# Column tiles by pairs in seven block products instead of eight, in a hybrid decoder step

## The chip, the cores and the metric

The kernel runs on one core of one Trainium2 chip. The metric is device time in microseconds (us). Engines are named as in the profile: PE is TensorE (PEld is its weight load), DVE is VectorE, ACT is ScalarE, POOL is GpSimd and SP is SyncE. SP issues most weight loads, POOL most other DMAs; each issues its queue in order.

## The reference

One layer of a decoder that runs stick-breaking attention and a gated short convolution side by side. The input is 528 prompt tokens (16 learned meta tokens and 512 others) and 32 sample tokens (8 sequences of 4), 560 in all, 2048 wide.

```python
h = rmsnorm(x, g_pre)
q, k, v, ga, cb, cc, ch, gc, ma, mc = jnp.split(h @ w_in, split_offsets(), axis=-1)
a = attend(q, k, v, b_sb).reshape(bsz, t, D_ATTN) * jax.nn.silu(ga)
u = cc * ch
u_ext = jnp.concatenate([conv_hist.astype(u.dtype), u], axis=1)
c = cb * causal_conv(u_ext, w_conv, b_conv) * jax.nn.silu(gc)
merged = (jax.nn.sigmoid(ma + b_gate[:D_MODEL]) * (a @ w_pa)
          + jax.nn.sigmoid(mc + b_gate[D_MODEL:]) * (c @ w_pc))
y = x + rmsnorm(merged @ w_out, g_post)
```

`w_in` is 2048 x 12288 float32: the eight parts q to gc are 1024 wide, ma and mc 2048 each. `w_pa` and `w_pc` are 1024 x 2048, `w_out` is 2048 x 2048. Attention has 8 heads of 128. Prompt queries read earlier prompt keys. The queries of a sample sequence read 512 past keys, in four pages of 128 that a page table names, and its earlier new keys. `A[t,s] = sigmoid(z_ts) * prod_{s<j<t} (1 - sigmoid(z_tj))` takes the place of a softmax. The convolution is depthwise with three taps. Outputs are y, the new keys and values, and the last two rows of u, for prompt and samples.

## The kernel before

**Products.** Every large product is made in two-part float32: an operand is split into `hi`, a rounded fp32r copy (ACT), and `lo`, the rest (DVE subtracts). Three matmuls, hi by hi, lo by hi and hi by lo, give one product. `weights` (L180) loads a block of 1024 x 128 of a weight on SP's queue into a `raw` buffer, ACT casts it (L188) and DVE subtracts (L189). `raw` has three buffers (L67), `hi` and `lo` four each (L68). `gemm_into` (L193) runs over two ranges of tokens, over all contraction tiles of 128, and over the three matmuls (L201). The activations h are stationary in SBUF as `h_hi` and `h_lo` (16 contraction tiles x 560 tokens each), with the tokens on the columns of the matmul. `proj` (L216) computes a column tile, 128 columns of h @ w_in: two weight blocks, 2 x 16 x 3 = 96 matmuls of 272 tokens or so, into two of three `mm` banks of PSUM.

**Stages.** (1) Norm of x, split of h (L98 to L244). (2) The gate `ga` of all heads, then head by head k, v, q and prompt attention (L335); the attention of a head runs beside the projections of the next, its result goes to `a_scr` in DRAM. (3) The output gates: 16 x 2 column tiles of ma and mc, a sigmoid each, both to `gate_scr` in DRAM (L659). (4) The conv: `conv_in` (L481) makes u and the three taps of a channel tile out of its cc and ch tiles; a second loop (L683) multiplies with silu(gc) and cb, and keeps the eight results in SBUF as `c_raw`. Tile 0 is made ahead, behind the last head (L516), before that head's pool closes. In the second loop a is read back from `a_scr` and split to `a_hl` (L697), two tiles in each of its last four rounds. (5) `c_raw` is split to `c_hl` (L705), which takes the memory of `h_hi`. Then for two output tiles at a time a @ w_pa and c @ w_pc, with the gate read back from `gate_scr` (L715 to L732); the merged result is split as m. (6) The output product: 288 tokens with weights stationary (L773), the others with m stationary (L812), with norm and residual. It begins on the DMA of x rows into memory that `a_hl` leaves.

**Decode.** The attention of the samples is a generator, `decode_steps` (L537), of which `dec_step` runs a piece. Logits: for each of 32 pages a key tile of 128 keys x 1024; for two of four tokens DVE multiplies a whole page by the query row, broadcast to all partitions (L553), and ACT sums by head (L556); for the other two DVE multiplies and sums by head (L560). One page per column tile of the gates. Then softplus, running sums and exponentials, and the value pages through PE (L631), between the conv's tiles. Its result `a_s` goes into the sample columns of `a_hl`.

**Order.** The program is written for a scheduler: instructions have the priority of their place in the text, each engine's queue is laid out ahead by a simulated timeline, later work fills the gaps of earlier work once its buffers are free, and buffers of a tag go round among their tiles. A pool that is opened after another is closed uses the same memory, so its first writes wait for the last readers there. The order in a queue is then fixed.

The lines that the change and the prediction's steps touch are those named, and the pool sizes:

```python
wraw = ctx.enter_context(tc.tile_pool(name="wraw", bufs=3))   # L67
whl = ctx.enter_context(tc.tile_pool(name="whl", bufs=4))     # L68
```

## Time and profile before

| what | value |
|---|---|
| median of 3 runs | 1734.3 us (1733.22 to 1734.79) |
| span of the profiled execution | 1736.9 us, 2.6 us above that median |
| PE busy | 1706.4 us, 12764 matmuls |
| DVE, ACT, POOL busy | 842.8, 744.7, 202.2 us |
| heads, up to the last output | about 66 to 543 us |
| gates, decode logits beside the first 250 us | 543 to 943 us |
| conv and value pages | 943 to 1332 us |
| w_pa, w_pc | 1332 to about 1529 us |
| output product, norm | about 1529 to 1737 us |
| HBM read, written | 225.42, 22.36 MB |

The span goes from the first to the last instruction of one profiled execution. A profiled execution has no other time of its own, so the span stands for it. [...]

### The profile page before, as it was taken

How to read it: one execution, taken by the hardware profiler on the slowest of the kernel's cores; microseconds unless marked ns; L12 is line 12 of the kernel's file. 1: busy time of each engine (PE TensorE's matmuls, PEld its weight loads, DVE VectorE, ACT ScalarE, POOL GpSimd, SP SyncE). 2: the span in 40 equal slices, each digit the busy share in tenths (PEclk: the TensorE clock that was granted, in tenths of full speed). 3: DMA queues.
4: the chain of work that ended last, by engine and by line, in shares of the span. 5: the costliest groups of instructions: out<-in, count | busy, mean ns of one | idle time of the engine just before them, and what ended most of it. 6: DMA issues, size and time to landing. Idle time of an engine off the chain costs nothing.

```text
span 1736.9 us, 32151 instructions
## 1 busy us (share of the span) xinstructions
PE 1706.4 (98%) x12764; PEld 1637.0 (94%) x12764; DVE 842.8 (49%) x2092; ACT 744.7 (43%) x2026; POOL 202.2 (12%) x345
## 2 busy tenths in 40 slices
PE   5999999999999999999999999999999999999997
PEld 4999999999999999999999878899999999999986
DVE  7322554554445999996123222242224554444464
ACT  4322555455454999886223111132223222244543
POOL 5000222122111111111001111010000000000010
PEclk9999999999999999999999999999999999999999
DMA  6333333333325777774343444343233444567584
GB/s 191 94 110 116 88 99 93 87 88 98 99 82 192 247 257 253 248 244 148 111 120 102 166 160 149 121 139 91 80 98 85 137 127 133 164 166 184 174 260 153
DMA packets 302057, 249.87 MB, mean 144 GB/s; under 512 B 9181, under 2 KB 272145, under 8 KB 298721
## 3 DMA queue, kind: packets, MB, share of 16 engines
q1 hardware_dynamic: 278992, 161.89, 32.0%
q0 software_dynamic: 22912, 85.91, 14.2%
q8 instruction: 100, 1.64, 0.4%
q14 instruction: 51, 0.42, 0.1%
q10 hardware_dynamic: 2, 0.01, 0.0%
HBM read 225.42 MB, written 22.36 MB: 143 GB/s over the span
## 4 chain that ended last, share of the span: by engine, by line
PE 95%; DVE 2%; DMA 2%; ACT 0%; issue 0%; SPq 0%; POOLq 0%; POOL 0%; ACTq 0%; DVEq 0%
PE mm L201 83%; PE z L631 2%; PE z L830 2%; PE mm L830 2%; PE z L450 1%; DMA raw<-in_w_out 1%; PE o L460 1%; PE z L396 1%; PE o L830 1%; DMA raw<-in_w_in 1%; DVE hn L164 0%; PE tp L830 0%; PE tp L316 0%; DVE h_lo L177 0%; PE z L785 0%; DVE rtmp L120 0%
## 5 line engine op out<-in xcount | busy, mean ns | idle before, releaser
L201 PE MATMUL mm<-h_hi,wlo 128*128 128x272 f32 (+4 forms) x3072 | 894.1, 291 | 0.0
L201 PE MATMUL mm<-h_hi,whi 128*128 128x272 f32 (+4 forms) x3072 | 892.9, 291 | 0.0
L201 PE MATMUL mm<-h_lo,whi 128*128 128x272 f32 (+4 forms) x3072 | 888.1, 289 | 0.3 <-DVE h_lo L177 0.2
L201 PEld LDWEIGHTS mm<-h_hi,whi 128*128 128x128 f32 x3072 | 580.7, 189 | 9.3 <-issue 6.7
L201 PEld LDWEIGHTS mm<-h_hi,wlo 128*128 128x128 f32 x3072 | 580.0, 189 | 4.1 <-issue 3.4
L201 PEld LDWEIGHTS mm<-h_lo,whi 128*128 128x128 f32 x3072 | 579.2, 189 | 4.8 <-issue 3.4
L189 DVE TENSOR_TENSOR wlo<-raw,whi 128x1024 fp32r<-128x1024 f32 x252 | 308.4, 1224 | 493.7 <-ACT whi L188 492.3
L188 ACT CAST whi<-raw 128x1024 fp32r<-128x1024 f32 x256 | 269.0, 1051 | 518.0 <-PE mm L201 499.8
L556 ACT ACTIVATE junk<-pr 128x128 f32<-128x128 f32 x512 | 150.7, 298 | 7.1 <-DVE pr L553 4.3
L560 DVE CUSTOM_DVE_ANT_0 prod<-page,qb 128x128 f32<-128x128 f32 x512 | 116.2, 285 | 1.0 <-DMA qb<-q_scr 1.0
L201 PE MATMUL mm<-m,whi 128*128 128x288 f32 x512 | 105.8, 301 | 0.0
L556 ACT ACTIVATION_READ_ACCUMULATOR junk<-pr 128x1 f32 x512 | 97.2, 190 | 0.0
L201 PE MATMUL mm<-c_hl,whi 128*128 128x272 f32 x512 | 96.8, 287 | 0.0
L201 PE MATMUL mm<-a_hl,whi 128*128 128x272 f32 x512 | 96.7, 288 | 0.0
L201 PEld LDWEIGHTS mm<-m,whi 128*128 128x128 f32 x512 | 84.0, 193 | 0.0
L553 DVE TENSOR_TENSOR pr<-page,qb 128x1024 f32<-128x1024 f32 x64 | 78.0, 1220 | 6.2 <-ACT junk L556 5.7
L201 PEld LDWEIGHTS mm<-c_hl,whi 128*128 128x128 f32 x512 | 80.7, 188 | 0.0
L201 PEld LDWEIGHTS mm<-a_hl,whi 128*128 128x128 f32 x512 | 80.5, 189 | 0.0
L201 PE MATMUL mm<-m,wlo 128*128 128x288 f32 x256 | 76.6, 299 | 0.0
L201 PE MATMUL mm<-c_hl,wlo 128*128 128x272 f32 x256 | 74.2, 290 | 0.0
L201 PE MATMUL mm<-a_hl,wlo 128*128 128x272 f32 x256 | 73.9, 289 | 0.0
L804 DVE TENSOR_TENSOR wlo<-raw,whi 128x1024 fp32r<-128x1024 f32 x32 | 39.1, 1224 | 38.4 <-ACT whi L803 37.9
(289 smaller groups left out, 1641.6 us busy)
## 6 DMA issues: line engine op xcount, KB each, us to landing
raw<-in_w_in SPq DMA_DIRECT2D x192, 512.0 KB, 3.9
raw<-in_w_out SPq DMA_DIRECT2D x64, 512.0 KB, 4.0
qb<-q_scr POOLq DMA_DIRECT2D x16, 1024.0 KB, 7.1
page<-in_cache_k POOLq DMA_DIRECT2D x32, 512.0 KB, 6.0
page<-in_cache_v POOLq DMA_DIRECT2D x32, 512.0 KB, 5.4
gate_scr<-gt POOLq DMA_DIRECT2D x16, 544.0 KB, 4.6
gt<-gate_scr POOLq DMA_DIRECT2D x16, 544.0 KB, 5.1
raw<-in_w_pa SPq DMA_DIRECT2D x16, 512.0 KB, 3.9
```

The costliest lines, as they stand in the source:

```text
L188: act.copy(hi, raw)
L189: lo_eng.tensor_sub(lo, raw, hi.bitcast(F32))
L201: pe.matmul(o, lhsT=w, rhs=r[:, t0:t1], start=(k == 0 and n == 0), stop=(k == nk - 1 and n == 2))
L396: pe.matmul(zt[:m, c0:c0 + n], lhsT=l[:, s0:s0 + m], rhs=r[:, ts:ts + n], start=(c0 == 0 and i == 0), stop=(i == 2), skip_group_check=True)
L450: pe.matmul(o, lhsT=l, rhs=x, start=False, stop=(i == len(ops) - 1), skip_group_check=True)
L460: pe.matmul(ot[:, ts - NMETA:ts - NMETA + n], lhsT=l[:m, st, :], rhs=x[:m, c0:c0 + n], start=False, stop=(g == GROUPS[-1] and i == 2), ski ...
L553: dve.tensor_mul(pr, kt, qb[0][:, t, :])
L556: act.activation(junk, pr[:, h * P:(h + 1) * P], AF.Copy, accum_out=z_all[:, pg, b, h, t:t + 1])
L560: dve.tensor_tensor_reduce(out=prod, in0=kt[:, h * P:(h + 1) * P], in1=qb[t // 2][:, t % 2, h * P:(h + 1) * P], scale=1.0, scalar=0.0, op0 ...
L631: pe.matmul(po[hf][32 * j:32 * (j + 1), :], lhsT=lhs, rhs=rhs, start=(pg == 0), stop=(pg == NPG), tile_position=(0, 32 * j), skip_group_ch ...
L804: dve.tensor_sub(lo, raw, hi.bitcast(F32))
L830: pe.matmul(po[i], lhsT=l, rhs=r, start=(k == 0 and q == 0), stop=(k == KD - 1 and q == 2))
```

## The change

**Tokens.** They are laid out in two halves of 280, each with 8 meta tokens ahead of 272 others. In every product the two ranges then have the same width: 280, 274 (272 and two before) or 272. The meta tokens are put back in front where keys and values are copied out (`nparts`).

**Pairs.** `pair(c, n)` computes two neighbouring column tiles for both halves of the tokens as a 2 x 2 block product: two blocks of contraction (1024 each) by two column tiles of the weight, and two blocks of contraction by two halves of the tokens. It uses the Winograd form with seven block products instead of eight. A block product is 8 contraction tiles x 3 matmuls. Sums of weight blocks are made on DVE (four passes over 128 x 1024 a pair, partly in place), and seven blocks are split instead of four. Sums of token blocks are made once (`diff`, `t_split`): three new split blocks of 8 x 274 columns, and the block (0, 1) of h is overwritten by a difference. The partial results accumulate in three PSUM banks with copies between (ACT, and two subtractions of DVE). The conv's cc, ch, gc, cb go by pairs (16 pairs), then ma and mc from tile 2 on (14 pairs). Four gate tiles, 0 and 1 of ma and mc, stay whole and run while the token sums are made.

**Order.** After the heads: four gate tiles, four conv pairs of channels (`conv_pair`), gate pairs. The heads' pool is closed before the first of these. Conv results go to `c_scr` in DRAM and are read back to `c_hl` when h is done. Then all 16 tiles of c @ w_pc, each multiplied by its gate and written back to `gate_scr`; then a is read back and split to `a_hl`; then all 16 tiles of a @ w_pa, with the sum. These loads share two buffers (tag `gt` of the pool `g3`).

**Decode.** Key pages are loaded in halves of 512 columns, once for each two tokens (twice the key traffic), in 32 steps of four half pages; a step has either the ACT sums or the DVE sums. `dec_group` runs a step behind four of every five pairs, 24 in all; the eight others and the rest of the decode run in the w_pc loop, two steps a tile. `v_new` goes through DRAM.

**Sizes.** `wraw` 3 to 5, `whl` 4 to 3, and the SBUF kept for DMA descriptors is 4096 bytes a partition.

```diff
-    wraw = ctx.enter_context(tc.tile_pool(name="wraw", bufs=3))
-    whl = ctx.enter_context(tc.tile_pool(name="whl", bufs=4))
+    wraw = ctx.enter_context(tc.tile_pool(name="wraw", bufs=5))
+    whl = ctx.enter_context(tc.tile_pool(name="whl", bufs=3))
...
+    def pair(c, n):
+        c1, c2, k1, k2 = slice(c, c + P), slice(c + P, c + 2 * P), slice(0, 1024), slice(1024, 2048)
+        w11, w21, w22, w12 = (w_load(win[k, m]) for k, m in ((k1, c1), (k1, c2), (k2, c2), (k2, c1)))
...
+        def product(o, w, rhs, start, stop):
+            hi, lo = w
+            for k in range(8):
+                rh, rl = rhs(k)
+                for m, (l, r) in enumerate(((hi, rh), (hi, rl), (lo, rh))):
+                    pe.matmul(o, lhsT=l[:, k, :], rhs=r, start=(start and k == 0 and m == 0),
+                              stop=(stop and k == 7 and m == 2), skip_group_check=True)
...
+        x, q, y = mm_ps()[:, :n], mm_ps()[:, :n], o_ps()[:, :n]
+        s = sp2.tile([P, 8, P], F32, name="s")
...
+        product(x, w_split(w11), rb(0, 0), True, False)
+        dve.tensor_add(s, w21, w22)
+        product(q, w_split(s), rb(0, 1), True, False)
+        act.activation(y, x, AF.Copy, scale=-1.0)
+        dve.tensor_add(s, s, w11)
+        product(y, w_split(s), rt(0), False, False)
+        s5 = tmp("s5")
+        act.copy(s5, q)
+        product(x, w_split(w12), rb(1, 0), False, True)
+        s2 = tmp("s2")
+        act.copy(s2, y)
+        yield 0, 0, x
+        dve.tensor_add(w21, w21, w11)
+        product(y, w_split(w21), rt(1), False, False)
+        c22 = tmp("c")
+        dve.tensor_sub(c22, y, s5)
+        yield 1, 1, c22
+        dve.tensor_add(s, s, w12)
+        product(q, w_split(s), rb(1, 1), False, True)
+        c12 = tmp("c")
+        dve.tensor_sub(c12, q, s2)
+        yield 0, 1, c12
+        product(y, w_split(w22), rt(2), False, True)
+        yield 1, 0, y
...
     c_hl = tok.tile([P, KD, TQ], F32R, tag="A", name="c_hl")
     for k in range(8):
+        cr = g3.tile([P, 2, TQ], F32, tag="gt", name="cr")[:, 0, :]
+        pool.dma_start(cr, c_scr[k])
+        split_evac(c_hl[:, k, :], c_hl[:, 8 + k, :], cr, cr)
...
+    for j in range(KD):
+        cs = slice(j * P, (j + 1) * P)
+        gt = g3.tile([P, 2, TQ], F32, tag="gt", name="gt")[:, 1, :]
+        pool.dma_start(gt, gate_scr[j][:, 1, :])
+        oc = gemm(weights([w_pc[0][:, cs]]), lambda k: (c_hl[:, k, :], c_hl[:, 8 + k, :]), QH)
+        for ob, s in qparts(oc):
+            dve.tensor_mul(gt[:, s], ob, gt[:, s])
+        pool.dma_start(gate_scr[j][:, 1, :], gt)
+        dec_step(2)
+    dec_step(2)
...
+    for k in range(8):
+        ar = g3.tile([P, 2, TQ], F32, tag="gt", name="ar")[:, 0, :]
+        pool.dma_start(ar[:, 0:PQ], a_scr[k])
+        dve.tensor_copy(ar[:, PQ:TQ], a_s[:, k, :])
+        split_evac(a_hl[:, k, :], a_hl[:, 8 + k, :], ar, ar)
```

More of the change, by code (lines that the diff above doesn't have):

```diff
@@ L37 @@
 EPS = 1e-6
+SCRATCH = 4096
 LNEXP = "natural_log_exp_and_others"
@@ new lines, in dec_step, with dec_group, w_load @@
+            if dec_at[0] in ("end", until) and dec_at[0] is not None:
+                return
+            dec_at[0] = next(dec, "end")
+    n_group = [0]
+    def dec_group():
+        n_group[0] += 1
+        if n_group[0] % 5:
+            dec_step(1, "logits")
+    gctx = ExitStack()
+    gp = gctx.enter_context(tc.tile_pool(name="gates", bufs=2))
+    sp2 = gctx.enter_context(tc.tile_pool(name="sums", bufs=1))
+    def w_load(src):
+        raw = wraw.tile([P, 8, P], F32, tag="raw", name="raw")
+        nc.sync.dma_start(raw, src.rearrange("(k p) c -> p k c", p=P))
+        return raw
@@ new lines, in hybrid_step_kernel @@
+    for i in range(0, 8, 2):
+        conv_pair(i)
+    for j in range(2, KD, 2):
+        for w, c in ((0, COL_MA), (1, COL_MC)):
+            gs = [gp.tile([P, 2, HU], F32, tag="cv", name="g", bufs=3).rearrange("p a b -> p (a b)")[:, 0:TQ] for _ in range(2)]
+            for m, half, b in pair(c + j * P, HQ):
+                act.activation(gs[m][:, by_query(m, half)], b, AF.Sigmoid, bias=gate_bias(j + m, w))
+            for m in range(2):
+                gate_out(j + m, w, gs[m])
+            dec_group()
@@ new lines, in hybrid_step_kernel @@
+    m2 = ap_.tile([P, KD, TQ], F32R, tag="m2", name="m2")
+    for j in range(KD):
+        cs = slice(j * P, (j + 1) * P)
+        gt = g3.tile([P, 2, TQ], F32, tag="gt", name="gt")
+        pool.dma_start(gt, gate_scr[j])
+        oa = gemm(weights([w_pa[0][:, cs]]), lambda k: (a_hl[:, k, :], a_hl[:, 8 + k, :]), QH)
+        mt = m1 if j < 8 else m2
+        for ob, s in qparts(oa):
+            dve.tensor_mul(gt[:, 0, s], ob, gt[:, 0, s])
+            dve.tensor_add(gt[:, 0, s], gt[:, 0, s], gt[:, 1, s])
+            split_evac(mt[:, j % 8, s], mt[:, 8 + j % 8, s], gt[:, 0, s], gt[:, 0, s])
```

383 lines of the change are left out of this document (210 added, 173 removed).

## The prediction, made before the changed kernel was run

> **What bounds the kernel now.** I read the page of the profile first: busy times, then the chain of work that ended last.
>
> ```profile
> span 1736.9 us, 32151 instructions
> ...
> PE 1706.4 (98%) x12764; PEld 1637.0 (94%) x12764; DVE 842.8 (49%) x2092; ACT 744.7 (43%) x2026; POOL 202.2 (12%) x345
> ...
> PE 95%; DVE 2%; DMA 2%; ACT 0%; issue 0%; SPq 0%; POOLq 0%; POOL 0%; ACTq 0%; DVEq 0%
> PE mm L201 83%; PE z L631 2%; PE z L830 2%; PE mm L830 2%; PE z L450 1%; DMA raw<-in_w_out 1%; PE o L460 1%; PE z L396 1%; PE o L830 1%; DMA raw<-in_w_in 1%; DVE hn L164 0%; PE tp L830 0%; PE tp L316 0%; DVE h_lo L177 0%; PE z L785 0%; DVE rtmp L120 0%
> ```
>
> PE is on the path for 95% of the span, and the column-tile matmuls of L201 are nearly all of it. A matmul less is therefore time won, as long as the others keep up. Whether they do I read by stage: decode logits beside gates, gates alone, the end of the conv, the start of the output product.
>
> ```profile
> core 0: us, PE busy (x) PEld busy (x) DVE busy (x) ACT busy (x) POOL busy (x), PEclk, DMA share, GB/s
> 560.00:640.00 80.00, 80.00 (x637) 80.00 (x636) 77.06 (x373) 74.00 (x401) 9.71 (x18) 1.00 0.79 266
> 800.00:943.00 143.00, 143.00 (x1137) 143.00 (x1136) 34.67 (x33) 47.26 (x59) 6.03 (x10) 1.00 0.41 117
> 1147.00:1330.00 183.00, 183.00 (x1455) 183.00 (x1454) 54.84 (x69) 41.91 (x54) 4.41 (x8) 1.00 0.35 102
> 1535.00:1590.00 55.00, 52.15 (x377) 51.84 (x376) 22.07 (x23) 26.18 (x70) 5.14 (x10) 0.94 0.78 193
> ```
>
> One matmul takes 183 / 1455 = 0.1258 us, and 143 / 1137 gives the same. In the first row DVE is 96% busy and PE still loses nothing: that will be the state of all pairs.
>
> **The part removed.** A pair of column tiles took 2 x 96 matmuls; seven products of 8 contraction tiles by 3 take 168. There are 16 conv pairs and 14 gate pairs: 30 x 24 x 0.1258 = **-90.6 us**, and a pair takes 168 x 0.1258 = 21.1 us of PE. The first two gate tiles of each kind stay whole. The conv blocks had 274 and 272 columns and now have 274: nothing.
>
> **What the pairs add on DVE and ACT.** Four weight splits become seven, with four sums more, all 128x1024. DVE operations overlap at their ends, so I take start to start, not duration:
>
> ```profile
> 602.86 0.28 DVE L560 CUSTOM_DVE_ANT_0 prod<-page,qb 128x128 f32<-128x128 f32 x1
> 603.07 0.08 DVE L560 DVE_READ_ACCUMULATOR2_ANT z_all<- 128x1 f32 x1
> 603.07 0.28 DVE L560 CUSTOM_DVE_ANT_0 prod<-page,qb 128x128 f32<-128x128 f32 x1
> ...
> 603.71 1.22 DVE L189 TENSOR_TENSOR wlo<-raw,whi 128x1024 fp32r<-128x1024 f32 x1
> 604.85 0.28 DVE L560 CUSTOM_DVE_ANT_0 prod<-page,qb 128x128 f32<-128x128 f32 x1
> ```
>
> A weight operation costs 1.14, a decode product 0.21. PSUM blocks cost 0.44, less 0.08 overlap = 0.36:
>
> ```profile
> L691 DVE TENSOR_TENSOR c_raw<-mm,gc x16: 433/442/443, 1157.1 to 1332.5; 128x272 f32<-128x272 f32 x16
> ```
>
> A gate pair needs 11 x 1.14 + 2 x 0.36 = 13.3 us. A 512-wide decode multiply, on the line between 272 and 1024 columns, costs 0.61, so a decode step is 8 x 0.61 = 4.9 (the half whose sums ACT makes) or 32 x 0.21 = 6.8; 24 steps over 30 pairs add 4.7 a pair. Gate pair: **18.0 of 21.1**. The conv adds, per column tile:
>
> ```profile
> L503 DVE SCALAR_TENSOR_TENSOR c_raw<-u,wcv,c_raw x24: 241/494/746, 974.2 to 1139.7; 128x512 f32<-128x512 f32 x12, 128x32 f32<-128x32 f32 x12
> L500 DVE TENSOR_SCALAR c_raw<-u,wcv x12: 295/422/548, 972.4 to 1136.9; 128x512 f32<-128x512 f32 x6, 128x32 f32<-128x32 f32 x6
> ...
> L493 DVE TENSOR_TENSOR u<-mm,cc x8: 435/444/445, 521.1 to 1130.0; 128x274 f32<-128x274 f32 x8
> L494 DVE TENSOR_TENSOR u<-mm,cc x8: 408/408/409, 527.5 to 1136.0; 128x240 f32<-128x240 f32 x8
> L495 DVE TENSOR_TENSOR u<-mm,cc x8: 181/182/184, 527.8 to 1136.3; 128x32 f32<-128x32 f32 x8
> ```
>
> Each less 0.08: 0.36 + 0.33 + 0.10 + 0.08 for two stray columns, and 0.69 + 2 x 0.82 for the taps, 3.2 a tile. Four conv pairs: 44 x 1.14 + 8 x 0.36 + 2 x 3.2 + 8 x 0.36 (silu and cb) + 4 x 4.7 = **81.1 of 84.5**. Full to 96%, as in the row 560 to 640. ACT:
>
> ```profile
> 613.67 1.05 ACT L188 CAST whi<-raw 128x1024 fp32r<-128x1024 f32 x1
> 614.62 0.30 ACT L556 ACTIVATE junk<-pr 128x128 f32<-128x128 f32 x1
> ...
> 614.93 0.29 ACT L556 ACTIVATE junk<-pr 128x128 f32<-128x128 f32 x1
> ```
>
> Seven casts of 0.95, seven evacuations near 0.4, and 32 x 0.31 in every other step: some 14 of 21.1. PE's cover is buffers: three hi/lo slots let a split run two products (6 us) ahead, and an in-place sum waits for the split before it. A decode step is emitted ahead of the next pair's splits, so it is served first; a late split leaves PE waiting. Bounds for the pair stages: 0 by the first row, +46 if operations don't overlap (rival C). I take **+10**, near the row that shows the same load.
>
> **Setting up.** Thirteen DVE passes over 8 x 274 columns (2192 / 1024 x 1.14 = 2.4 us each, 32 us in all) form the token sums beside four gate tiles of 12.1 us with 9 us of splits. Hidden, but for the block of h overwritten in place once the last of these tiles has read it: 0 to 5, **+2**. The heads' pool now closes before anything else of the conv starts, and the gate result's slot lies in its memory. The last head runs from its logits to its output:
>
> ```profile
> 508.91 0.69 ACT L286 ACTIVATE e<-z,bsb 128x512 f32<-128x512 f32 x1 [0.87 <-PE z L396]
> ```
> ```profile
> 543.13 0.69 DVE L464 TENSOR_TENSOR sg<-o,sg 128x512 f32<-128x512 f32 x1 [1.68 <-PE o L460]
> ```
>
> 34 us, which 27 us of column tiles fill now. Three PSUM blocks hold 18 us of them, and the rest waits for a slot: 0 to 10, **+6**. With three hi/lo slots instead of four, the second weight unit of a head's tile is split only after 75% of the tile before; 3 us of slack stay: 0 to 12, **+3**.
>
> **The two refills.** The conv result goes through DRAM. It used to lie in SBUF when its split began; now eight tiles are loaded into two slots, each load behind the split of the one two before. This pattern stands in the trace as the loads of a_scr, hidden there:
>
> ```profile
> 1155.56 0.55 POOL L700 DMA_DIRECT2D arl<-a_scr  x1 [5.86 <-DVE arl L701]
> 1156.40 0.55 POOL L700 DMA_DIRECT2D arl<-a_scr  x1 [0.29 <-DVE arl L701]
> 1160.38 0.55 POOL L700 DMA_DIRECT2D arl<-a_scr  x1 [3.44 <-DVE arl L701]
> 1163.03 0.55 POOL L700 DMA_DIRECT2D arl<-a_scr  x1 [2.10 <-DVE arl L701]
> ```
> ```profile
> L305 ACT CAST c_hl<-c_raw x8: 641/642/646, 1333.3 to 1337.2; 128x544 fp32r<-128x544 f32 x8
> L306 DVE TENSOR_TENSOR c_hl<-c_raw,c_hl x8: 714/716/720, 1334.6 to 1339.4; 128x544 fp32r<-128x544 f32 x8
> ```
>
> A slot turns in 4.8 to 6.6 us. c_hl needs h_hi's memory, free when the last pair's sixth product ends, 3 us ahead of PE's need. Two tiles are loaded by then; three turns of 5.1 us for the other six end 14 us after PE's need. PE then has its second half (3 us) left: done at 17.6 instead of 6.0, **+12** (0 to 16). Before, the w_pa gemms covered this split; that cover is gone. In front of w_pa the same happens to a_hl, and worse: its slots are those of the w_pc results, the last freed only after its multiply and store, and the last sequence's attention must be done. By the same turns the eighth split ends 23 us after PE's need: **+21** (8 to 27). The trace has one idle of this kind:
>
> ```profile
> 1578.83 0.87 PE L785 MATMUL z<-ident,orw 128*96 128x128 f32 x3 [2.85 <-ACT orw L782]
> ```
>
> After 2.85 us idle the granted clock of 1535 to 1590 is 0.94: 0.06 x 55 = 3.3 us. Two refills: **+6**. [...]
>
> **The w_pc stage** now writes its result back and reads it again for w_pa, beside the V pages:
>
> ```profile
> page<-in_cache_v POOLq DMA_DIRECT2D x32, 512.0 KB, 5.4
> gate_scr<-gt POOLq DMA_DIRECT2D x16, 544.0 KB, 4.6
> gt<-gate_scr POOLq DMA_DIRECT2D x16, 544.0 KB, 5.1
> ```
>
> At half the size I estimate 3 + 3 us, and 4 us of holding in a slot; two slots give 12.1 per turn. It just fits, and not where page loads stretch it, for stores, loads and pages share POOL's queue: 0 to 30, **+8**. In the output product five raw buffers may hide the stall just shown (2.85 + 3.3), but the x rows that were loaded before it now wait for a_hl's memory and land in it: -6 to +5, **-3**.
>
> Sum: -90.6 + 10 + 2 + 6 + 3 + 12 + 21 + 6 + 8 - 3 = -25.6. The profiled execution goes from a span of 1736.9 to 1711.3; the runs' median lies 2.6 below that span: **1708.7 us**.
>
> **The rivals.** A, the sum: 50%. B, the refills mostly hide because splits and loads are reordered (4 and 8 us instead of 12 and 21 with their clock, and 6 for all else): 1734.3 - 90.6 + 18 = 1662 us. For it: PE's clean rows at full DVE; against: two slots cannot prefetch eight tiles. 17%.
>
> C, DVE becomes the bound and the kernel is slower. Place: the pairs. If each operation costs its whole duration because it waits on ACT's cast, a gate pair is 11 x 1.22 + 0.9 = 14.3, four conv pairs 68.6, and the 24 decode steps average (5.5 + 11.7) / 2 = 8.6: 4 x 68.6 + 14 x 14.3 + 206 = 680 us against 634 of PE. That is +46 in place of +10: 1745 us. It decides when the mean pair needs over 21.1 us of DVE. The row 560 to 640 speaks against it, since its operations do overlap; the alternation of sum, cast and split speaks for it. 17%. [...]
>
> D, the decode is late. Eight of 32 logit steps are emitted only in the w_pc stage: 32 loads at 6 us over three buffers, 64 us; an estimate of 25 us for softplus and exponentials (eight passes of 1024 columns at 1.1 to 1.2 us, then four dependent pages); 32 V pages, 16.8 MB at 266 GB/s, 63 us. That is 152 us against 97 of w_pc and 35 of L631 (2% of the span). PE then waits 20 us in front of w_pa, 1729 to 1733 us, no change. For it: DVE has no room in the conv pairs to run ahead; against: 3 us of room in each gate pair. 16%.
>
> **From cases to numbers.** Below 0.2% (3.5 us) this kernel can't be told from no change. Faster: B, nearly all of A and part of D, 72%. The same: most of D, 10%. Slower: C and the tails, 18%. The range reaches from B's 1662, cut for its weight, to past C: 1668 to 1750; A's own range is 1690 to 1728.
>
> **What would show it.** 17.4% fewer matmuls in the pairs is 720 fewer in the count. The stage of the pairs should last 634 to 650 us with DVE at 90% or more; idle of PE above 15 us there, released by DVE's lo, means C. At the first c_hl and a_hl matmuls PE's idle should be released by the splits, and POOL's loads should follow each other in turns of 5 us; if both are under 5 us, B. PE waiting for a_s is D. I am wrong if the w_pc stage or the last head loses more than 30 us.

## The result, and the profile after

The changed kernel takes **1763.7 us** (median of 4 runs, 1761.3 to 1769.6) against 1733.8 (4 runs) for the kernel before: ratio 1.0178, 95% interval 1.0161 to 1.0196. It is slower by 30 us; 1708.7 was predicted, with a range of 1668 to 1750. (The expectations below write VectorE, ScalarE, TensorE and GpSimd for DVE, ACT, PE and POOL.)

The page of the changed kernel: busy times, DVE and the granted clock in 40 slices, the chain that ended last by engine and by line.

```profile
span 1768.0 us, 32089 instructions
...
PE 1676.3 (95%) x12044; PEld 1574.7 (89%) x12044; DVE 1134.5 (64%) x2448; ACT 902.5 (51%) x2231; POOL 309.1 (17%) x530
...
DVE  7622554555546899989998999998541126654564
...
PEclk8899999999997999999999999999899999999998
...
PE 63%; DVE 13%; DMA 10%; issue 9%; ACT 4%; POOL 1%; SPq 0%; DVEq 0%; POOLq 0%; ACTq 0%
PE mm L203 40%; PE mm L704 5%; PE o L704 5%; DMA raw<-in_w_in 4%; DMA kpage<-in_cache_k 4%; PE z L631 3%; DVE wlo L682 3%; DVE prod L553 2%; PE z L995 2%; PE mm L995 1%; DVE pr L544 1%; PE z L459 1%; ACT whi L681 1%; ACT junk L550 1%; PE o L469 1%
```

The 720 matmuls are gone (12764 to 12044), but PE holds only 63% of the chain instead of 95%; DVE has 13% of it, and loads of `w_in` and of K pages 4% each. DVE stands at 8 and 9 tenths through the pairs, slices 14 to 28. The stages, each row a stretch with its length, busy times, granted clock and DMA share: conv pairs; gate pairs; start of the c_hl refill, its end, the rest of w_pc; a_hl refill, the rest of w_pa; output product.

```profile
577.00:961.40 384.40, 359.74 (x2716) 353.20 (x2715) 355.84 (x933) 254.74 (x803) 65.63 (x115) 0.97 0.56 169
961.40:1263.00 301.60, 296.50 (x2337) 294.44 (x2335) 270.98 (x723) 216.94 (x645) 54.88 (x98) 1.00 0.65 198
...
1263.00:1268.00 5.00, 0.00 (x0) 0.00 (x0) 1.23 (x1) 1.79 (x3) 1.62 (x3) 0.86 0.97 314
1268.00:1295.00 27.00, 21.16 (x99) 18.44 (x100) 17.34 (x32) 19.48 (x26) 12.26 (x19) 0.65 0.61 202
1295.00:1447.00 152.00, 150.80 (x865) 100.59 (x863) 32.31 (x64) 19.75 (x21) 31.45 (x59) 1.00 0.63 201
1447.00:1471.00 24.00, 15.18 (x78) 13.07 (x79) 9.02 (x20) 6.26 (x10) 4.93 (x10) 0.79 0.48 139
1471.00:1558.00 87.00, 87.00 (x694) 87.00 (x693) 55.75 (x105) 27.13 (x45) 7.39 (x14) 1.00 0.58 186
...
1558.00:1768.00 210.00, 197.28 (x1201) 179.28 (x1199) 105.50 (x137) 97.25 (x204) 21.16 (x38) 0.98 0.66 194
```

PE needs 16 x 21.1 = 338 us for the conv pairs and takes 384; the gate pairs need 296 and take 302. (Here and below the stretch of the conv pairs ends where the last conv result's store is issued, 1 to 7 us behind PE's last conv matmul.) The granted clock of 0.97 over 384 us is some 11 us of that loss. Where each stage ends is seen from the first and last starts of the matmuls, by line:

```profile
L704 PE MATMUL mm<-h_hi,whi x960: 282/288/432, 577.1 to 1259.2; 128*128 128x272 f32 x141, 128*128 128x274 f32 x51
...
L203 PE MATMUL mm<-c_hl,whi x512: 282/288/788, 1268.1 to 1445.4; 128*128 128x272 f32 x171
L203 PE MATMUL mm<-a_hl,whi x512: 283/288/597, 1448.2 to 1557.7; 128*128 128x272 f32 x171
```

The pairs last from 577.1 to 1262.9 (3.7 us, the rest of the last pair, behind the start listed last): 685.8 us where PE needs 634.0.

What PE waited for in the conv pairs (us in total, times, longest) names no transfer, only differences, casts and splits, the work of ACT and DVE; and ACT's casts in turn waited for a sum of DVE (first row). DVE itself, idle for 28.5 of the 384 us, stood 11.2 in front of weights (second row) and 8.5 in front of K pages and q rows:

```profile
ACT whi L681 <- DVE s L717: 16.6, 7, 6.6
...
DVE s L714 <- DMA raw<-in_w_in: 11.2, 7, 2.8
PE o L704 <- DVE c L728: 10.1, 5, 3.0
...
PE mm L704 <- ACT whi L681: 6.7, 9, 1.8
...
PE o L704 <- ACT whi L681: 2.8, 3, 1.7
...
PE o L704 <- DVE wlo L682: 2.3, 3, 1.0
```

And the decode's products on DVE (with the sum's read-out): the last starts at 1229.6, so all 32 logit steps, not 24, ran inside the pairs.

```profile
L553 DVE CUSTOM_DVE_ANT_0 prod<-kpage,qb x512: 274/284/293, 603.0 to 1229.6; 128x128 f32<-128x128 f32 x171
```

Three theories for the pairs: DVE has too much to do (1); the chain of sum, cast and split is too long for its slots (2); weights come late behind the K pages (3). For the w_pc stage: the turn of two slots, or the V pages.

### The profile page after: what moved, and what is told of

The parts are those of the page before. It is cut to its first block, busy times and chain, and to the rows that moved or that the text cites. A ratio compares the mean times of both kernels' runs of the same rounds, so it can differ in the third digit from the quotient of the medians.

```text
span 1768.0 us, 32089 instructions
## 1 busy us (share of the span) xinstructions
PE 1676.3 (95%) x12044; PEld 1574.7 (89%) x12044; DVE 1134.5 (64%) x2448; ACT 902.5 (51%) x2231; POOL 309.1 (17%) x530
## 4 chain that ended last, share of the span: by engine, by line
PE 63%; DVE 13%; DMA 10%; issue 9%; ACT 4%; POOL 1%; SPq 0%; DVEq 0%; POOLq 0%; ACTq 0%
PE mm L203 40%; PE mm L704 5%; PE o L704 5%; DMA raw<-in_w_in 4%; DMA kpage<-in_cache_k 4%; PE z L631 3%; DVE wlo L682 3%; DVE prod L553 2%; PE z L995 2%; PE mm L995 1%; DVE pr L544 1%; PE z L459 1%; ACT whi L681 1%; ACT junk L550 1%; PE o L469 1%
## 5 line engine op out<-in xcount | busy, mean ns | idle before, releaser
L203 PE MATMUL mm<-h_hi,whi 128*128 128x272 f32 (+3 forms) x1152 | 338.1, 294 | 5.9 <-ACT g L749 5.5
L203 PE MATMUL mm<-h_lo,whi 128*128 128x272 f32 (+3 forms) x1152 | 337.5, 293 | 0.1
L203 PE MATMUL mm<-h_hi,wlo 128*128 128x272 f32 (+3 forms) x1152 | 336.8, 294 | 0.0
L704 PE MATMUL mm<-h_hi,whi 128*128 128x272 f32 (+1 forms) x960 | 279.3, 291 | 8.4 <-ACT whi L681 8.2
L704 PE MATMUL mm<-h_lo,whi 128*128 128x272 f32 (+1 forms) x960 | 277.4, 289 | 0.1
L704 PE MATMUL mm<-h_hi,wlo 128*128 128x272 f32 (+1 forms) x960 | 275.4, 290 | 1.1 <-DVE wlo L682 1.1
L704 PE MATMUL o<-t_hi,whi 128*128 128x272 f32 (+1 forms) x720 | 213.6, 297 | 17.2 <-DVE c L728 12.8
L203 PEld LDWEIGHTS mm<-h_hi,wlo 128*128 128x128 f32 x1152 | 219.8, 191 | 0.2
L704 PE MATMUL o<-t_hi,wlo 128*128 128x272 f32 (+1 forms) x720 | 212.3, 295 | 2.7 <-DVE wlo L682 2.7
L704 PE MATMUL o<-t_lo,whi 128*128 128x272 f32 (+1 forms) x720 | 211.3, 294 | 0.0
L704 PEld LDWEIGHTS mm<-h_hi,wlo 128*128 128x128 f32 x960 | 180.5, 189 | 1.6 <-DVE wlo L682 1.5
```

Source lines behind the costliest of these rows:

```text
L203: pe.matmul(o, lhsT=w, rhs=r[:, t0:t1], start=(k == 0 and n == 0), stop=(k == nk - 1 and n == 2))
L704: pe.matmul(o, lhsT=l[:, k, :], rhs=r, start=(start and k == 0 and m == 0), stop=(stop and k == 7 and m == 2), skip_group_check=True)
```

## Experiments: what the pairs lose

**Without the logits' work.** The products and sums are left out, every load stays.

```diff
-                            for t in range(2):
+                            dve.tensor_copy(z_all[:, pg, b, 4 * hf, 2 * tp_:2 * tp_ + 1], kt[:, 0:1])
+                            for t in range(0):
```

> Leaves out the products and sums of the decode logits (the 512-wide multiplies, the 128-wide products with their sums on VectorE, the sums on ScalarE); every load of q and K pages stays, and one column of each page is copied. Theory 1, VectorE has too much to do in the conv pairs (35 us of demand above TensorE's 338, as all logit steps run ahead into the pairs): conv pairs 338 to 345 us instead of 385, gate pairs 296 to 299 instead of 303, kernel 1712 to 1722 us instead of 1763.7. Theory 2, the chain of sum, cast and split over three hi/lo slots is late whatever else VectorE does: conv pairs stay above 370, kernel 1745 to 1760. Theory 3, weight loads are late beside the K pages: conv pairs stay above 370 as well, since the pages are still loaded.

Measured 1750.0 us (1.0103 of before, 1.0075 to 1.0131). Gate pairs clean at 295, conv pairs still 371. By the number that is theory 2 or 3, but the conv pairs, three later stretches of 32 us, and DVE's wait for pages show another state than the changed kernel's:

```profile
575.00:946.00 371.00, 350.27 (x2712) 347.19 (x2711) 273.20 (x453) 149.21 (x227) 105.14 (x185) 0.99 0.74 234
863.00:895.00 32.00, 30.98 (x243) 30.62 (x242) 22.07 (x30) 13.93 (x22) 3.22 (x6) 1.00 0.58 183
895.00:927.00 32.00, 32.00 (x256) 31.94 (x255) 28.54 (x45) 14.14 (x24) 2.04 (x4) 1.00 0.33 96
927.00:959.00 32.00, 32.00 (x257) 32.00 (x256) 23.01 (x24) 13.97 (x18) 1.14 (x2) 1.00 0.41 121
```

```profile
DVE z_all L542 <- DMA kpage<-in_cache_k: 39.4, 44, 2.2
```

Nothing paces the pages now; they all run through in the first 300 us (up to 323 GB/s in a stretch of 32 us), and once they are through, PE is clean. DVE is busy for only 273 us, but stands 39.4 us with the copy of a column in front of a page, with later work behind it in its queue. So two more runs: the work without loads, and neither.

**One page for all, and no logits at all.**

```diff
+            qt = d1.tile([P, 2, 512], F32, name="qb", bufs=1)
+            pool.dma_start(qt, q_scr[0:2, 0:512].unsqueeze(0).broadcast_to([P, 2, 512]))
+            kt = d1.tile([P, 512], F32, name="kpage", bufs=1)
+            page_load(kt, kc, 0, 0, slice(0, 512))
             for hf in range(2):
...
-                            kt = d1.tile([P, 512], F32, name="kpage", bufs=3)
-                            page_load(kt, kc, b, pg, cs)
```

In the second of the two kernels a step does nothing:

```diff
+            for _ in range(32):
+                yield
```

> All products and sums of the decode logits stay on VectorE and ScalarE, but they read one K page and one pair of q rows that are loaded once; the 127 other page loads and 31 other q loads are left out, so the logits come out as those of one page. Without the logits' work (first experiment) the pairs still took 667 us against 688 while 88 MB were loaded in the stage of the conv pairs, and ran at TensorE's pace once the pages were through. If the loads are the larger cause (weights late behind pages, VectorE held in front of a page with a split queued behind): conv pairs 338 to 355 us instead of 385, kernel 1728 to 1740. If VectorE's load is: conv pairs 370 to 385, kernel 1745 to 1762.

> Leaves out the decode logits whole: no q or K page loads, no products, no sums (the logits are zeros; softplus, exponentials and V products stay). If logits and their loads together are all that the pairs lose: conv pairs 338 to 343 us, gate pairs 294 to 298, kernel 1708 to 1716. If the chain of sum, cast and split over three hi/lo slots and five raw slots loses by itself: conv pairs over 350, kernel above 1722.

Measured 1772.8 us (1.0211, 1.0189 to 1.0233) with one page, 1721.5 (0.9917, 0.9896 to 0.9939) with none. The stretches, conv pairs and gate pairs, first one page, then none:

```profile
575.70:973.80 398.10, 370.58 (x2746) 360.35 (x2744) 388.43 (x1002) 331.88 (x1228) 13.94 (x27) 0.97 0.32 94
973.80:1265.00 291.20, 290.34 (x2302) 289.90 (x2303) 241.49 (x653) 143.45 (x219) 15.09 (x28) 1.00 0.43 129
```

```profile
576.70:918.80 342.10, 341.96 (x2709) 341.49 (x2708) 266.18 (x325) 149.38 (x227) 12.62 (x24) 1.00 0.36 106
918.80:1213.00 294.20, 294.20 (x2341) 294.20 (x2341) 195.06 (x179) 139.28 (x196) 15.13 (x28) 1.00 0.42 128
```

Theory 2 falls: without logits the pairs run at PE's pace (636.5 us), over the same three slots. Theory 3 falls as the only cause: without a single page load the conv pairs are the slowest yet, 398 us, with DVE busy for 388 of them. Without loads to wait for, more steps run ahead: 24.3 in the conv pairs, against 17.4.

**VectorE or ScalarE.** With one page, PE's waits were mostly for ACT's casts (17.2 of the 27.5 us that it stood idle in the conv pairs), so each engine's share is taken away, one at a time, in the kernel with one page.

```diff
-                                        junk = d1.tile([P, P], F32, name="junk", bufs=1)
-                                        act.activation(junk, pr[:, hs], AF.Copy, accum_out=out)
+                                        if h == 0:
+                                            act.activation(z_all[:, pg, b, 4 * hf, 2 * tp_ + t:2 * tp_ + t + 1], pr[:, 0:1], AF.Copy)
```

```diff
-                                        prod = d1.tile([P, P], F32, name="prod", bufs=2)
-                                        dve.tensor_tensor_reduce(
-                                            out=prod, in0=kt[:, hs], in1=qt[:, t, hs], scale=1.0, scalar=0.0,
-                                            op0=ALU.mult, op1=ALU.add, accum_out=out)
+                                        pass
```

> As the run with one page (no loads of K pages and q rows in the pairs), and ScalarE's 512 sums over 128 columns are left out; VectorE's multiplies and product sums stay (half of the logits come out as zeros or single products). ScalarE loses 158 us of work, VectorE none. If VectorE's load is the cause: pairs 675 to 690 us as with one page (689.5), kernel 1758 to 1775. If ScalarE's sums hold back the casts: pairs 640 to 655, kernel 1722 to 1740.

> As the run with one page, and VectorE's 512 product sums are left out (half of the logits are zeros); the 512-wide multiplies and ScalarE's sums stay. VectorE's demand in the pairs falls by 16 x 6.7 = 107 us to 515 of 634, ScalarE's is unchanged. If VectorE's load is the cause: pairs 640 to 655 us, kernel 1722 to 1740. If ScalarE's sums are: pairs 675 to 690, kernel 1758 to 1775.

Measured 1773.7 us (1.0233, 1.0212 to 1.0253) without ACT's sums: nothing gained. 1729.4 (0.9967, 0.9954 to 0.9979) without DVE's products. Conv pairs without the one, then without the other:

```profile
574.60:971.00 396.40, 361.97 (x2722) 353.27 (x2721) 390.82 (x1011) 168.63 (x355) 14.01 (x27) 0.97 0.32 93
```

```profile
575.10:928.90 353.80, 348.60 (x2729) 345.32 (x2728) 334.36 (x452) 327.41 (x1240) 13.93 (x27) 1.00 0.36 105
```

ACT busy for half as long (169 us) leaves the conv pairs at 396; with ACT at 327 but DVE at 334 they take 354. In the kernel with one page it is DVE; that a cast comes late where the sum that it takes does, as in the changed kernel, is argued.

**Eight products instead of seven**, all else as changed (but the block of h stays as it is).

```diff
-        product(x, w_split(w11), rb(0, 0), True, False)
-        dve.tensor_add(s, w21, w22)
...
+        for m in range(2):
+            outs = gemm(weights(win_srcs(c + m * P)), h_rhs, [(HC - n, HC), (T - n, T)])
+            for half, o in enumerate(outs):
+                yield m, half, o
```

> Undoes the seven products alone: each column tile of a pair is again 96 whole-depth matmuls per token half from two splits, no weight sums, no block of h overwritten; the order, the slots, the pages and the conv via DRAM stay as in the changed kernel. TensorE then needs 24.15 us a pair, 724.6 for the 30 pairs, and VectorE 8 us a pair less. Theory 1 (VectorE's load): the pairs run clean, 725 to 730 us instead of 688, kernel 1800 to 1806; what is left over the kernel before, about 66, is the cost of order and refills. Theory 3 (loads late, whatever the products): the pairs lose 30 us or more again, kernel above 1825. If the refills and the stage of w_pc are better off without the pairs, below 1790.

Measured 1860.0 us (1.0717, 1.0699 to 1.0735), 96 more than with seven products, which cost 90.6 us of PE less; the rest of the change takes 125 away. The pairs take 779 us where PE needs 724.6, so they lose 54 us, as much as with seven, although the weight sums are gone: that is what was expected if loads come late whatever the products. All 32 steps ran in the conv pairs (the last product at 977), faster than pages came, and DVE was busy for only 282 us of the 388 from 577 to 965: its products stood 44 us in front of a page, with splits behind them in the queue, and PE 29 us for those. DVE's steps can thus hold PE up in two ways, by their work and by standing in front of a page.

**Weight sums on GpSimd.** `dve.tensor_add` becomes `pool.tensor_add` in the four sums.

> The four weight sums of a pair run on GpSimd instead of VectorE (about 2.7 us each instead of 1.2, 10.8 in a pair of 21.1). Theory 1: VectorE's demand in the conv pairs falls from 355 to about 282 us, below TensorE's 338; conv pairs 338 to 350 us, kernel 1718 to 1735. Theory 2 (the chain's length): each sum reaches its split 1.5 us later, four times a pair; conv pairs 390 us or more, gate pairs 310 or more, kernel 1770 to 1810. Theory 3: no change, within 5 us of 1763.7, or worse if page loads queue behind the sums.

Measured 1900.7 us (1.0957, 1.0939 to 1.0975): further off than any theory had it, the pairs 816 us. A stretch of the trace (start, duration) shows why; the last row is the pairs as a whole:

```profile
701.02 0.28 DVE L553 CUSTOM_DVE_ANT_0 prod<-kpage,qb 128x128 f32<-128x128 f32 x1
701.19 2.40 POOL L730 TENSOR_TENSOR s<-s,raw 128x1024 f32<-128x1024 f32 x1 [0.95 <-DVE wlo L682]
701.23 2.51 DVE L553 CUSTOM_DVE_ANT_0 prod<-kpage,qb 128x128 f32<-128x128 f32 x1
703.66 1.22 DVE L682 TENSOR_TENSOR wlo<-raw,whi 128x1024 fp32r<-128x1024 f32 x1
```

```profile
576.90:1392.60 815.70, 696.57 (x5050) 678.49 (x5048) 718.64 (x1537) 472.35 (x1447) 445.67 (x330) 0.94 0.49 153
```

A DVE product that takes 0.28 us takes 2.51 when it starts 0.04 after a POOL add of 2.40, and ends 0.15 after that. Over the whole run the 512 products take 0.47 us in the mean (0.28 in the changed kernel), the 128 multiplies over 512 columns 1.09 (0.68) and the 120 splits of raw blocks 1.74 (1.22). DVE is busy for 718.6 us in the pairs; before the move it was 626.8, of which the 120 sums at 1.14 were 137. So by the difference an estimate of 229 us of DVE's time goes to the adds on POOL, 1.9 each in place of 1.14.

**Fewer steps in the pairs, in three ways.** From here on with the slots of the next section (six `gt`, ten V pages; 1720.4 us by themselves). First, the last 8 or 12 steps take their slots from a pool opened in the w_pc loop, in memory that is free only after the pairs; and, in another kernel, two slots for c22/c12 and five for K pages.

```diff
+        with tc.tile_pool(name="dec1", bufs=2, side="right") as d1:
+            yield from logit_steps(d1, 3, order[:24])
+        yield "early"
+        with tc.tile_pool(name="dec1b", bufs=2) as d1:
+            yield from logit_steps(d1, 8, order[24:])
```

> Six slots, ten V page slots, and the last 8 of the 32 logit steps take their slots from memory that is free only after the pairs, so 24 run in the pairs. If the pairs lose by VectorE's load (49 us with 32 steps, 2 with none): at 24 steps its demand is 622 - 47 = 575 of 634 us, and the pairs lose 10 to 28, 644 to 662 us instead of 684; the stage of w_pc grows by 5 to 20 for the 8 steps ahead of the softplus; kernel 1692 to 1712 against 1720 with the slots alone. If the loss is one of head-of-line waits behind page loads, in proportion to the steps: pairs 672, kernel 1715 to 1725, no gain.

> The same with 12 late steps and 20 in the pairs. VectorE's demand falls to 552 of 634 us: pairs lose 5 to 15, 639 to 650 us. The stage of w_pc has 12 steps, 70 us of VectorE, ahead of softplus and V products: TensorE has 97 us of column tiles to cover 20 + 70 + 25 us, so it waits some 20 us more than with 8 late steps; kernel 1700 to 1720, slower than with 8. If the stage of w_pc hides them: 1685 to 1695.

> Six slots and ten V page slots, and beside them two slots for the difference blocks (c22, c12) instead of one, five K page slots instead of three; all 32 steps in the pairs. If single slots cause TensorE's waits for the c22 difference (10 us in the conv pairs) and VectorE's for pages (8 us): pairs 660 to 672 us instead of 684, kernel 1705 to 1712. If these waits are only where a late VectorE shows: within 4 us of 1720.

All three missed: 1735.9 us (1.0003, 0.9992 to 1.0013), 1763.9 (1.0171, 1.0143 to 1.0199) and 1731.8 (0.9980, 0.9967 to 0.9992). With 8 or 12 late steps the conv pairs still held 17.4 steps and took 377 and 379 us; only the gate pairs got fewer, and they had little to lose. Steps run as far ahead of their place in the program as the page slots allow: five page slots put 20.5 into the conv pairs, which then took 393 us. So DVE's load in the conv pairs was not lowered as meant, and these runs don't decide between the theories. In the w_pc stage the late steps held PE up, 16.0 us in front of the first new key sums in the kernel with 8.

So each step was held back: its q load waits for the pair that it is emitted behind, because a column of that pair's result is copied into its slot first. Then 14 steps are emitted in the conv pairs; or 10, with 8 beside the last four heads; or 6, with 12 there.

```diff
+                        act.copy(qt[:, 0, 0:1], pace[0])
                         pool.dma_start(qt, q_scr[r0:r0 + 2, cs].unsqueeze(0).broadcast_to([P, 2, 512]))
...
     for h in range(H):
         head(h)
+        if h >= 4:
+            dec_step(2, 'heads')
```

> Six slots and ten V page slots; the q load of each logit step waits for the pair behind which the step is emitted (a one-column copy into its slot), 14 steps in the conv pairs, 18 in the gate pairs. If the loss is VectorE's load in the conv pairs (250 us of its own work plus 5.85 a step, against 338 of TensorE): demand falls from 355 to 332, conv pairs 350 to 368 us instead of 380, gate pairs 298 to 310, kernel 1697 to 1714 against 1720. If it is page loads or latencies, whatever the count: pairs within 5 us of 684, kernel 1716 to 1726.

> The same holding back, and 8 of the 32 steps run beside the last four heads; 10 in the conv pairs, 14 in the gate pairs. VectorE's demand in the conv pairs is 250 + 59 = 309 of 338 us: conv pairs 342 to 356 us, gate pairs 296 to 302, heads 0 to 8 longer, kernel 1682 to 1704. If the count in the conv pairs does not matter: conv pairs 370 or more, kernel above 1712. If page loads in GpSimd's queue hold back the masks of the heads: heads over 15 us longer, kernel above 1700 although the pairs gain.

> The same with 12 steps beside the last four heads, 6 in the conv pairs, 14 in the gate pairs. Demand in the conv pairs 250 + 35 = 285 of 338 us: conv pairs 338 to 348 us, gate pairs 296 to 302, heads 0 to 15 longer, kernel 1674 to 1704. If the count does not matter: as in the run with 8, conv pairs 370 or more.

Measured 1738.3 us (1.0021, 1.0008 to 1.0034), 1707.9 (0.9845, 0.9812 to 0.9878) and 1709.0 (0.9850, 0.9829 to 0.9872). The first missed: against the kernel with the slots alone its conv pairs gained 6 us and its gate pairs lost 7, where DVE was now busy for 275 of 311 us; the pairs together stayed as they were, as expected if the count does not matter. It is slower than that kernel because steps ran on behind the pairs (the last product at 1301) and the stretch from there to w_pa took 168 us instead of 156. The other two are 4 and 5 us above their ranges; the pairs came out as expected, but heads (9 and 15 us) and the w_pc stage (7) paid more. Conv pairs of the three:

```profile
574.00:948.40 374.40, 353.78 (x2727) 349.27 (x2727) 334.50 (x801) 230.59 (x690) 53.90 (x95) 0.99 0.51 156
```

```profile
584.00:936.00 352.00, 346.98 (x2727) 344.50 (x2726) 312.53 (x653) 207.21 (x558) 41.84 (x74) 1.00 0.49 147
```

```profile
591.00:935.70 344.70, 343.69 (x2713) 342.35 (x2712) 293.60 (x539) 183.84 (x424) 32.01 (x58) 1.00 0.45 134
```

Conv pairs by the steps in them. Steps are counted from the products on DVE and the sums on ACT that start in the stage, 32 to a step:

| steps in the conv pairs | DVE busy, us | length, us (PE needs 338) | kernel |
|---|---|---|---|
| 0 | 266 | 342 | no logits |
| 6.0 | 294 | 345 | held back, 12 beside heads |
| 9.5 | 313 | 352 | held back, 8 beside heads |
| 13.6 | 335 | 374 | held back |
| 17.4 | 356 | 377 to 384 | as changed; 8 late; 12 late; ten V page slots |
| 20.5 | 373 | 393 | five page slots |
| 24.3 | 388 | 398 | one page |

The loss begins between 294 and 313 us of DVE work in a stage of 338, at about 90%; from 356 on the stage is as long as DVE's work and 10 to 30 us. Fewer steps are also fewer page loads, so the table does not part the two. Beside it stand the kernels that have one without the other: 334 us of DVE work take 354 without page loads (no products, one page) and 374 with them (held back), and 273 us take 371 where pages come unpaced and 342 (266 us) where none come. So the logit steps in the pairs are the cause of the pairs' loss, and DVE's work in them is enough for it by itself; how much of the changed kernel's 46 us in the conv pairs is DVE's work and how much its standing in front of loads isn't shown.

## Experiments: the refills and the w_pc stage

**Six slots for the tag `gt`**, then also **ten V page slots** instead of five; and, by itself, four hi/lo and four raw slots.

```diff
-    g3 = g3ctx.enter_context(tc.tile_pool(name="g3", bufs=2))
+    g3 = g3ctx.enter_context(tc.tile_pool(name="g3", bufs=6))
...
-                        vt = d2.tile([P, DA], F32, name="vpage", bufs=5)
+                        vt = d2.tile([P, DA], F32, name="vpage", bufs=10)
```

> Six slots instead of two for the tiles of the refills, the w_pc results and the w_pa results. If the turn of a slot (load, split, next load) sets the refills and the stage of w_pc: the splits of c_hl take 10 to 14 us instead of 23, those of a_hl 10 instead of 20, the stage of w_pc 155 to 170 instead of 182; kernel 1730 to 1747. If the V pages, the decode's end or the granted clock set that stage: the refills alone gain, 5 to 12 us, kernel 1752 to 1759. If the block of h that c_hl overwrites and the last sequence's attention come too late anyway: within 3 us of 1763.7.

> Six slots as in the experiment on the refills, and ten slots instead of five for the V pages. In the kernel before, the V products came in bursts of 20 and took 41 us of TensorE; in the changed kernel nearly all come by fours, 59 us. If the arrival of the pages in five slots breaks them up: the V products take 41 to 47 us, the kernel 1726 to 1734 against 1744 with six slots alone. If the loads come no faster than 2 MB per 15 us anyway, or the column tiles between are what breaks them: 1740 to 1746.

> Four hi/lo slots instead of three and four raw slots instead of five, throughout; all else as in the changed kernel. If the pairs lose because a split runs only two products ahead (cover of 6 us): TensorE's waits for splits, 24 us in the conv pairs, fall below 10 with the clock's loss, conv pairs 350 to 365, heads 3 us shorter, kernel 1735 to 1750. If VectorE has too much to do in all: a deeper buffer only moves the wait, conv pairs 378 to 388, kernel 1755 to 1764. If the weights come late: four raw slots make it worse, above 1766.

Six slots: 1744.2 us (1.0054, 1.0038 to 1.0071), in the range for the slots' turn: the splits of c_hl take 12 us instead of 23, those of a_hl 10 instead of 20. Ten V page slots beside them: **1720.4 us** (0.9910, 0.9888 to 0.9932), faster than the kernel before and below the range expected, since w_pa gained as well: with the decode done earlier, a_hl was split before PE asked for it. The V products of the kernel before (two halves), the changed one, and this one, these instructions alone:

```profile
971.00:1055.00 84.00, 20.58 (x80) 4.26 (x80) 1.00 0.48 164
1055.00:1138.00 83.00, 20.58 (x80) 4.26 (x80) 1.00 0.43 139
```

```profile
1320.00:1432.00 112.00, 58.91 (x160) 11.23 (x160) 1.00 0.63 209
```

```profile
1313.00:1387.00 74.00, 41.47 (x160) 8.38 (x160) 1.00 0.69 242
```

41.2 us, 58.9, 41.5. Where the time goes stands in the changed kernel's timeline:

```profile
1321.15 3.62 PE L631 MATMUL z<-vpage,A_all 128*32 128x512 f32 x20
1330.44 1.90 PE L631 MATMUL z<-vpage,A_all 128*32 128x512 f32 x4
1333.86 1.90 PE L631 MATMUL z<-vpage,A_all 128*32 128x512 f32 x4
```

Twenty together take 3.62 us, 0.18 each; four of one page take 1.90, 0.47 each. The program puts the products of four sequences into four groups of 32 columns (`tile_position`); in these rows a product is cheap only where the pages of several sequences are there together, and why is not shown. With five slots, of which a group holds four, they come one by one; with ten the products take 41.5 us.

Four hi/lo and four raw slots: 1775.4 us (1.0236, 1.0212 to 1.0260), above the changed kernel, as theory 3 had it; but the profiled pairs (688.0 us) and the start of the pairs (578.7) hardly moved, so what the loss of a raw slot costs isn't located. More cover for a split gains nothing here, though with one raw slot fewer.

The quickest kernel of the study is the one with six slots, ten V page slots, 8 steps beside the heads and steps held back: 1707.9 us; the one with 12 beside the heads (1709.0) can't be told from it.

## Why the prediction was wrong

Step by step, against the profiled executions (1736.9 to 1768.0, +31.1):

| term | predicted | measured | from |
|---|---|---|---|
| PE in the pairs | -90.6 | -90.6 (96 when undone) | 720 matmuls |
| pairs beside it | +10 | +51.8 | 685.8 - 634.0 |
| to the pairs' start | +11 | +21.1 | 3456 column matmuls done at 577.1, before at 556.0 |
| c_hl refill, its clock, w_pc | +23 | +34.5 | 1262.9 to 1445.4, less 96.6, 41.2 and 10.2 |
| a_hl refill, its clock | +24 | +15.7 | 1445.4 to 1557.7, less 96.6 |
| output product | -3 | -1.7 | 210.0 against 211.7 |

The measured terms come to 30.8. The 10.2 is PE's other work (transposes, the decode's sums): between 556.0 and the output product at 1525.2 the kernel before has 969.2 us, of which 7296 column matmuls take 917.8 and the V products 41.2. The third term is read from the column matmuls alone, before and after; from the stretch up to the 192nd of them, before and after; and from the last stretch ahead of the pairs, with PE's longest wait there:

```profile
0.00:556.00 556.00, 470.93 (x3455) 455.44 (x3456) 1.00 0.36 106
```

```profile
0.00:577.20 577.20, 471.25 (x3456) 456.98 (x3456) 0.96 0.35 100
```

```profile
0.00:66.20 66.20, 47.99 (x290) 40.83 (x290) 45.33 (x71) 32.13 (x53) 24.25 (x21) 0.97 0.53 149
```

```profile
0.00:71.10 71.10, 51.82 (x290) 44.26 (x291) 55.64 (x75) 31.74 (x55) 25.56 (x21) 0.83 0.61 144
```

```profile
500.00:577.10 77.10, 68.01 (x464) 63.56 (x463) 43.66 (x45) 34.20 (x49) 7.40 (x15) 0.87 0.21 66
```

```profile
PE mm L203 <- ACT g L749: 5.5, 1, 5.5
```

**The step that failed** is "What the pairs add on DVE and ACT", in two places. "24 steps over 30 pairs add 4.7 a pair" took the emission for the pace. All 32 ran in the pairs, 17.4 of them in the conv pairs, where 12.8 were counted: four conv pairs then need 62.3 + 17.4 / 4 x 5.85 = 87.7 us of DVE, not 81.1, in 84.5. By its own durations the sum says that DVE is the bound. And "I take +10, near the row that shows the same load": that row of the kernel before (DVE 96% busy, PE clean) did not carry over. Here PE loses from about 90% on. The row had decode work that could wait and splits that were few; in a pair, seven splits and four sums are due in order. That this is the reason is argued, not shown. In place of +10 the pairs lost 51.8 us. That the logit steps are the cause is shown by the kernel without them (636.5 us for all pairs), and that DVE's work alone is enough by the runs with one page, without ACT's sums and without DVE's products. The sum also had nothing for DVE standing in front of loads, and nothing for the clock in the pairs (some 11 us).

**Mis-sized** is the term of the w_pc stage. 18 of its 34.5 us are the V products, 41.2 to 58.9, for which the sum had nothing: that five slots now break them up was not seen. The rest is, to within 3 us, the stretch of the c_hl refill: 5 us without a matmul, and 27 in which 99 matmuls (12.5 us) ran. The splits of c_hl took 23 us, up to 29 us after PE's need, where 14 were reckoned; the mechanism was right, and six slots halved it. PE's own waits for them were 6.7 us in all; another 4.3 in this stretch were in front of the decode's sums, behind the softplus, which shares DVE with the splits (first the stretch at the low clock, then that wait):

```profile
1266.60:1287.10 20.50, 13.36 (x46) 11.12 (x47) 12.78 (x23) 17.04 (x21) 9.62 (x15) 0.50 0.70 242
```

```profile
1283.96 1.22 PE L602 MATMUL z<-dr,neg_u 128*128 128x256 f32 x2 [4.30 <-DVE dr L302]
```

Of the clock, 21.16 busy us at 0.65 make 7.4, and in the a_hl refill 15.18 at 0.79 make 3.2, where a row of before gave 3.3 for each. In the c_hl refill the granted clock was 0.50 for 20.5 us on end, from 1266.6 to 1287.1.

The 21.1 us up to the pairs have three parts. The 192nd column matmul is past 4.9 us later than before (71.1 against 66.2 us, at a granted clock of 0.83 against 0.97); the sum had no term for the norm stage, the profiled executions of the other kernels with this beginning are 1 to 7 us late there too, and why is open. The heads between lose nothing (446.7 against 448.1 us), so the +3 for three hi/lo slots did not come. The last head loses 17.4. Its term has the right wait, 5.5 us of PE for the gate result's slot (6 predicted), but neither the other 3.6 us that PE stands idle in the last stretch nor the clock: 68.01 busy us at 0.87 are 8.8 more. The clock fell at 529.3, ahead of that wait, where the last head's attention had PE to itself: it was 1.00 from 500 to 529.3 and 0.50 from there to 545, with PE busy for 9.4 of those 15.7 us.

**What was right:** the matmuls (720 of 5760 are 12.5%, though, not the 17.4% that stands there), the last head's wait, the direction and the place of both refills, and the warning on the w_pc stage.

**The rivals.** C had the place and nearly the price, 46 against 51.8, at a chance of 17%. Its criterion, over 21.1 us of DVE in the mean pair, held for the conv pairs (355.84 / 16 = 22.2) and not for all thirty (626.8 / 30 = 20.9); its sign, PE idle for over 15 us behind DVE's `lo`, did not come (3.8 us over the pairs; most was for the differences and for ACT's casts). Its mechanism, that each operation costs its whole duration, fell: operations of 1.21 to 1.22 us still start 1.13 to 1.14 apart, in the changed kernel's pairs too. That the price came near is luck. Two rows of the conv pairs:

```profile
703.37 1.21 DVE L730 TENSOR_TENSOR s<-s,raw 128x1024 f32<-128x1024 f32 x1
704.50 0.28 DVE L553 CUSTOM_DVE_ANT_0 prod<-kpage,qb 128x128 f32<-128x128 f32 x1
```

D fell, as the logits were done before the w_pc stage, and left only the 4.3 us above; with 8 and 12 late steps it came about. B fell with two slots; with six and ten the a_hl refill did hide, and PE still stood 5.0 us for c_hl.

## What to carry to other kernels

Count an engine's work in the stage where it will run, with everything in it that waits for no one there: work that is emitted late runs as early as its buffers allow (here all 32 logit steps in the pairs, where 24 were emitted), and a deeper buffer lets more of it in (20.5 steps in the conv pairs with five page slots, 17.4 with three). An engine that feeds the bound one needs room to spare in each stage, here some 10% with page loads beside it (313 us of DVE work in a stage of 338 took 352, 335 took 374); on average over a longer stretch is not enough. An instruction that waits for a load can hold up the bound engine by what stands behind it in its queue: with eight products DVE's stood 44 us in front of pages, and PE 29 for the splits. When transfers move into a stage, look also at what their arrival does to the instructions that were fast only because their inputs came together, here the V products (41.2 to 58.9 us).

## What the runs showed of the hardware that was not expected

With the weight sums on POOL (adds of 128x1024), DVE's operations beside them were stretched: a product of 0.28 us took 2.51 beside an add of 2.40, and the mean product 0.47. The granted clock stayed at 0.50 for 20.5 us though PE was busy in 13.4 of them (1266.6 to 1287.1). The V products (32 columns of weights) cost 0.18 us each in a run of twenty over several sequences and 0.47 in a run of four over one. And K pages that nothing paces (up to 323 GB/s), with the copy of one column of each, cost the conv pairs some 29 us (371 against 342), though DVE was then only 74% busy (273 of 371); it stood 39.4 us in front of pages.
